# A transformer block on one core: the last products' snapshots and joins between the k tiles, and the gate g1 behind the output projection

## The chip, the core and the metric

The kernel runs on one core of a Trainium2 chip. A core has TensorE (PE in the rows) for matrix products, VectorE (DVE), ScalarE (ACT) and GpSimd (POOL) for the element work, and SyncE (SP), whose queue issues nearly all of the transfers between HBM and the on-chip memory SBUF here. Products collect in PSUM, in banks of 128 x 512 fp32. Each engine takes its instructions in a fixed order, and one that waits holds up all behind it on its engine. The metric is the time of one execution on the device, in microseconds.

## What is computed

A diffusion block on 1024 tokens of width 1024 in fp32. Cut to what matters here:

```python
mod = split(silu(c) @ w_ada + b_ada)            # sh1, sc1, g1, sh2, sc2, g2: one row of 1024 each
y   = sigmoid(ga) * (a_out @ w_branch_a) + sigmoid(gb) * (b_out @ w_branch_b)
x   = x + g1 * (y @ w_out)                      # output projection
h   = modulate(rmsnorm(x, norm2_g), sh2, sc2)
a, g = split(h @ w_ffn_in)                      # 1024 -> 2 x 2816
x   = x + g2 * ((silu(g) * a) @ w_ffn_out)      # 2816 -> 1024
return rmsnorm(x, final_norm_g)
```

Ahead of it stand the input projection, a gated linear attention (b_out) and a grouped MLP (a_out), which the change does not touch.

## The kernel before, in words

**High and low parts.** TensorE's fast fp32 form is coarser than fp32, so each operand X is split: `hi` is a rounded copy of X (a cast on ScalarE, L228 or L907) and `lo` is X - hi (a subtraction on VectorE, L229 or L908). A product is three matmuls, hi x hi, hi x lo and lo x hi (`PASS`). So each weight tile goes through a transfer (SyncE), a cast, a subtraction, and only then TensorE. `split_w` does that for weights, `parts_of` (L907, L908) for the tiles of the FFN.

**Who sets the order.** The program is written engine-free and a scheduler lays the instructions of each engine down in one fixed stream, roughly in the order in which the code emits them, as far as the buffers of the pools are free. Matmuls passed through `pe()` keep the program's order among themselves. So what is emitted early stands early in the queues of ScalarE, VectorE and SyncE, whether or not its inputs are there.

**Branch units and w_out.** For each of eight column blocks `fo`, a unit of 48 matmuls (L265) computes the gate, and another one a_out @ w_branch_a. At `fo` = 6 the row of g1 is spread over all partitions (`row_of`, L693 and L694), and `out_weights(0)` loads half of w_out in four tiles, multiplies each with that row (L837, two on GpSimd, two on VectorE) and splits them. The raw tiles come from the same small pool as the tiles of w_branch_a, so the load of the last unit waits until one of them is split. `project` then makes 24 matmuls per token tile and half (L880) and adds the result to x (L881). The second half is loaded by `out_weights(1)` in the same way. Behind each second half the token tile is normalised, and the transposed tiles feed the FFN.

**FFN in.** 22 blocks `fi` of 128 columns. A two-by-two block form with seven products stands for the eight, on sums of the weight's four quarters (S1 to S4, built in `weights_s`, L955 to L958) and of the activations. Behind each product stands element work that combines them (L987 to L1007); the results go to HBM (`actd`).

**FFN out.** Again seven products, P1, P7, P2, P6, P5, P4, P3 in this order, each over 11 k tiles (`quarter`, L1099 to L1101; P3 apart, L1166 to L1170). `prepared` loads a k tile's operands one ahead, combines them (L1074 to L1087) and splits them; a k tile is then 12 matmuls into four banks. All but P3 go k tile by k tile; P3 goes bank by bank, so its first bank wants all 11 tiles. Between the products stands the following, each piece for four token tiles:

- behind P1 and P7: a snapshot of the four banks by ScalarE (L1111, L1115)
- behind P2: `join`, that is multiply by the row of g2 and add to x (L1129, L1130)
- behind P6: add, subtract, multiply, add (L1138 to L1141)
- behind P5: add and `join` (L1158)
- behind P4: add, `join` and `finish`, the last normalisation (L1162, L1145 to L1154)
- behind each bank of P3: `join` and `finish`

In before all of it is emitted behind the product's last k tile and ahead of the next product's first. The row of g2 is made behind the loop over `fi`.

Of the kernel before, what the change touches and what calls it, by code (L numbers as in the profile page):

```python
# [1 line left out]

# [6 lines left out]
F32 = mybir.dt.float32  # L9
# [7 lines left out]
P = 128  # L17
T = 1024
TC = 256
D = 1024  # L20
# [12 lines left out]
def block_kernel(  # L33
# [796 lines left out]
    def out_weights(n):  # L830

        cols = slice(n * 512, (n + 1) * 512)
        parts = []
        for kp in range(KT // 2):
            raw = raw_w([P, 2, 512])
            nc.sync.dma_start(raw, w_out[kp * 256:(kp + 1) * 256, cols].rearrange("(k p) f -> p k f", p=P))
            (nc.vector if kp % 2 else nc.gpsimd).tensor_mul(raw, raw, g1r[:, cols].unsqueeze(1).to_broadcast([P, 2, 512]))  # L837
            parts.append(split_w(raw, [P, 2, 512], pool=True))
        return parts

# [29 lines left out]
    def project(n, tt, wo):  # L870
        cols = slice(n * 512, (n + 1) * 512)
        if n == 0:
            xt = slot([P, D])
            nc.sync.dma_start(xt, x[tt * P:(tt + 1) * P, :])
            x2.append(xt)
        xt = x2[tt]
        ps = bank()
        for k in range(KT):
            for i, (a, b) in enumerate(PASS):
                pe(nc.tensor.matmul(ps, yF.get(b, k, tt * P, P), wo[k // 2][a][:, k % 2, :], start=k == 0 and i == 0, stop=k == KT - 1 and i == 2))  # L880
        nc.vector.tensor_add(xt[:, cols], xt[:, cols], ps)  # L881
        if n == 1:
            xn = slot([P, D])
            rms_scaled(xt, xn)
            xns.append(xn)
            nc.sync.dma_start(x2d[tt], xt)
# [53 lines left out]
    def weights(fi, which=(0, 1)):  # L940
        got = []
        for i in which:
            w = raw_w([P, KT, P])
            nc.sync.dma_start(w, w_ffn_in[:, i * DFF + fi * P:i * DFF + (fi + 1) * P].rearrange("(k p) f -> p k f", p=P))
            got.append(w)
        return got

    def weights_a(va):
        hi, lo = split_w(va, [P, KT, P])
        return {"A11": (hi[:, 0:4, :], lo[:, 0:4, :]), "A12": (hi[:, 4:8, :], lo[:, 4:8, :])}  # L950
# [33 lines left out]
    def second(q):  # L984
        product(q["A"], q["ops"]["A12"], op_t["B21"], False)
# [43 lines left out]
    op_t["T1"] = moving(combined("tensor_sub", b12, b11, dve))  # L1029
    op_t["T4"] = moving(combined("tensor_sub", b21, t2, dve))  # L1030
    op_t["B22"] = moving(b22)
    for fi in range(NF):
        if fi < EARLY:
            if fi:
                weights_s(*weights(fi), quads[fi]["ops"], nc.vector)
            rest(quads[fi], fi)
        else:
            va, ga = weights(fi)
            q = {"ops": weights_a(va)}
            weights_s(va, ga, q["ops"], nc.gpsimd)  # L1040
            first(q)
            rest(q, fi, lambda: second(q))


    g2r = row_of(g2)
    sk = [slot([P, 2, 512]) for _ in range(KH // 2 + 1)]

    def act_q(k, t):
# [45 lines left out]
            t, now = operands(name, k + 1) if k + 1 < KH else None, t  # L1094
            yield parts_of(now)

    def quarter(name, banks, start):
        for k, o in enumerate(prepared(name)):
            for tt in range(4):  # L1099
                for i, (a, b) in enumerate(PASS):  # L1100
                    pe(nc.tensor.matmul(banks[tt], o[b][:, 0, tt * P:(tt + 1) * P], o[a][:, 1, :], start=start and k == 0 and i == 0, stop=k == KH - 1 and i == 2, skip_group_check=True))  # L1101

    def four():
        t = [slot([P, 2, 512]) for _ in range(2)]
        return [t[i // 2][:, i % 2, :] for i in range(4)]

    A, X = [gbank() for _ in range(4)], [bank() for _ in range(4)]
    quarter("P1", A, True)
    p1 = four()
    for tt in range(4):  # L1110
        nc.scalar.copy(p1[tt], A[tt])  # L1111
    quarter("P7", X, True)
    q7 = four()
    for tt in range(4):
        nc.scalar.copy(q7[tt], X[tt])  # L1115
    quarter("P2", A, False)
    fin = []
    fng, junkt = slot([P, D]), slot([P, 2, 512])
    junk = junkt[:, 0, :]
    nc.gpsimd.dma_start(fng, final_norm_g.partition_broadcast(P))  # L1120

    def residual(tt):
        xt = slot([P, D])
        nc.sync.dma_start(xt, x2d[tt])
        fin.append(xt)

    def join(xt, sl, src):
        t = tmp("gj")
        nc.vector.tensor_mul(t, src, g2r[:, sl])  # L1129
        nc.vector.tensor_add(xt[:, sl], xt[:, sl], t)  # L1130

    for tt in range(4):
        residual(tt)
        join(fin[tt], lh, A[tt])
    quarter("P6", X, False)
    u3 = four()
    for tt in range(4):
        nc.vector.tensor_add(u3[tt], X[tt], p1[tt])  # L1138
        nc.vector.tensor_sub(q7[tt], u3[tt], q7[tt])
        nc.vector.tensor_mul(q7[tt], q7[tt], g2r[:, rh])  # L1140
        nc.vector.tensor_add(fin[tt][:, rh], fin[tt][:, rh], q7[tt])  # L1141
    Y = [gbank() for _ in range(4)]
    quarter("P5", Y, True)

    def finish(tt):  # L1145
        xt = fin[tt]
# [6 lines left out]
            nc.vector.scalar_tensor_tensor(xt[:, sl], xt[:, sl], r[:, 0:1], fng[:, sl], op0=ALU.mult, op1=ALU.mult)  # L1153
            nc.sync.dma_start(out[tt * P:(tt + 1) * P, sl], xt[:, sl])  # L1154

    for tt in range(4):
        residual(4 + tt)
        nc.vector.tensor_add(u3[tt], Y[tt], u3[tt])  # L1158
        join(fin[4 + tt], rh, u3[tt])
    quarter("P4", X, False)  # L1160
    for tt in range(4):
        nc.vector.tensor_add(p1[tt], X[tt], p1[tt])  # L1162
        join(fin[4 + tt], lh, p1[tt])
        finish(4 + tt)

    o = list(prepared("P3"))  # L1166
    for tt in range(4):
        for k in range(KH):
            for i, (a, b) in enumerate(PASS):
# [35 lines left out]
```

## Time and profile before

| what | value |
|---|---|
| median of three runs | 1830.47 us (1828.61 to 1831.2) |
| the profiled execution | 1830.24 us |
| its span, first to last instruction | 1828.5 us |
| mean granted TensorE clock | 0.989 of full |
| w_branch_a's last unit ends, projection begins | 1058.59 us |
| FFN in ends, P1's first matmul | 1587.02 us |
| first matmul of P7, P2, P5, P3 | 1623.36, 1658.38, 1719.38, 1790.31 us |
| last matmul, end of span | 1820.41, 1828.5 us |

The profile is of one execution. Times are microseconds from the span's start. A timeline row gives a run of instructions of one form: its start, its length, the engine, the line, out <- in with partitions x elements, the count, and in brackets how long the engine had stood idle and what it waited for. Matmuls overlap, so the rate is read from the starts of rows and not from their lengths. The chain of waits is followed back from the last instruction: at each step the piece that released the next.

### The profile page before, as it was taken

The page shows a single profiled execution, that of the slowest core. Times are in us where ns is not written, and L with a number is a line of the kernel's source. Part 1 is how long each engine was busy: PE and PEld are TensorE (multiplying, and loading weights), DVE is VectorE, ACT ScalarE, POOL GpSimd, SP SyncE. Part 2 cuts the span into 40 slices and gives each one's busy share as a digit, 9 for nine tenths or more (in the row PEclk, how much of TensorE's full clock was granted, in tenths as well). Part 3 has the DMA queues.
Part 4 walks back from the last instruction along what each step waited for, and adds up shares of the span by engine and source line. Part 5 has one row for each costly group of instructions (what it writes and reads, how often), then busy time and mean ns, then how long its engine had stood idle before and what let it go on. Part 6 is the DMA issues. An engine that isn't in the chain of part 4 may idle for free.

```text
span 1828.5 us, 21986 instructions
## 1 busy us (share of the span) xinstructions
PE 1770.2 (97%) x8786; PEld 1478.2 (81%) x8786; DVE 982.2 (54%) x1386; ACT 600.4 (33%) x892; POOL 147.4 (8%) x145
## 2 busy tenths in 40 slices
PE   8899999999999999999999999989999999999898
PEld 3887888888887889988888788768888888777686
DVE  7687463553346525543322453885555455446786
ACT  6653342423211112132211222533333333345243
POOL 2220000000000000000000100011211211000001
PEclk9999999999999999999999999999999999999899
DMA  9501001011156448611111251242222222467382
GB/s 344 148 24 35 24 24 46 13 35 35 47 149 188 146 136 318 238 47 47 38 55 47 70 172 69 70 127 81 92 81 76 86 81 92 162 219 256 108 297 92
DMA packets 182870, 201.84 MB, mean 110 GB/s; under 512 B 8624, under 2 KB 132592, under 8 KB 182768
## 3 DMA queue, kind: packets, MB, share of 16 engines
q1 hardware_dynamic: 181952, 199.01, 33.6%
q0 software_dynamic: 720, 1.40, 0.3%
q8 instruction: 69, 1.13, 0.2%
q14 instruction: 33, 0.27, 0.0%
q10 hardware_dynamic: 96, 0.02, 0.0%
HBM read 168.94 MB, written 31.46 MB: 110 GB/s over the span
## 4 chain that ended last, share of the span: by engine, by line
PE 71%; DVE 4%; DMA 1%; issue 1%; ACT 1%; POOL 0%; DVEq 0%; POOLq 0%; ACTq 0%
PE m L265 28%; PE m L971 14%; PE g L971 6%; PE g L1101 5%; PE m L277 5%; PE m L1101 5%; PE m L880 5%; PE g L1170 2%; DVE s L908 1%; PE g L799 1%; DMA wr<-in_w_ffn_in_dram 1%; DVE s L916 0%; PE g L681 0%; DMA wr<-in_w_branch_a_dram 0%; DVE wlo L229 0%
## 5 line engine op out<-in xcount | busy, mean ns | idle before, releaser
L265 PE MATMUL m<-s,whi 128*128 128x512 f32 (+1 forms) x1856 | 571.5, 389 | 3.8 <-ACT whi L228 3.2
L265 PEld LDWEIGHTS m<-s,whi 128*128 128x128 f32 x1856 | 347.9, 189 | 75.3 <-ACT whi L228 4.1
L265 PE MATMUL m<-s,wlo 128*128 128x512 f32 (+1 forms) x928 | 360.1, 388 | 2.3 <-DVE wlo L229 2.3
L971 PE MATMUL m<-s,s 128*128 128x512 f32 x1320 | 309.5, 391 | 8.7 <-ACT q L991 3.8
L229 DVE TENSOR_TENSOR wlo<-wr,whi 128x1024 fp32r<-128x1024 f32 x106 | 129.7, 1225 | 344.7 <-ACT whi L228 311.8
L971 PEld LDWEIGHTS m<-s,s 128*128 128x128 f32 x1320 | 248.1, 189 | 64.1 <-ACT q L991 5.5
L228 ACT CAST whi<-wr 128x1024 fp32r<-128x1024 f32 x106 | 111.4, 1051 | 445.3 <-PE m L265 311.3
L277 PE MATMUL m<-whi,s 128*128 128x256 f32 x1152 | 218.1, 287 | 0.1
L265 PEld LDWEIGHTS m<-s,wlo 128*128 128x128 f32 x928 | 175.5, 189 | 37.6 <-DVE wlo L229 2.9
L277 PEld LDWEIGHTS m<-whi,s 128*128 128x128 f32 x1152 | 181.3, 192 | 4.5 <-issue 2.9
L277 PE MATMUL m<-wlo,s 128*128 128x256 f32 x576 | 164.4, 285 | 1.6 <-DVE wlo L229 1.6
L908 DVE TENSOR_TENSOR s<-wr,s 128x1024 fp32r<-128x1024 f32 x77 | 91.3, 1218 | 40.9 <-ACT s L907 40.4
L277 PEld LDWEIGHTS m<-wlo,s 128*128 128x128 f32 x576 | 110.2, 191 | 3.5 <-DVE wlo L229 2.0
L971 PE MATMUL g<-s,whi 128*128 128x512 f32 x352 | 108.4, 389 | 0.0
L907 ACT CAST s<-wr 128x1024 fp32r<-128x1024 f32 x77 | 78.3, 1050 | 60.5 <-DVE wr L1082 30.1
L1101 PE MATMUL g<-s,s 128*128 128x512 f32 x264 | 84.4, 402 | 11.3 <-DVE s L908 11.3
L908 DVE TENSOR_TENSOR s<-s,s 128x1024 fp32r<-128x1024 f32 x58 | 89.9, 1563 | 3.9 <-ACT s L907 3.9
L907 ACT CAST s<-s 128x1024 fp32r<-128x1024 f32 x58 | 60.4, 1053 | 89.0 <-DVE s L908 43.8
L880 PE MATMUL m<-s,s 128*128 128x512 f32 x384 | 87.5, 389 | 0.0
L1101 PE MATMUL m<-s,s 128*128 128x512 f32 x264 | 83.5, 398 | 0.7 <-DVE s L908 0.7
L880 PEld LDWEIGHTS m<-s,s 128*128 128x128 f32 x384 | 72.0, 188 | 14.9
L164 POOL TENSOR_TENSOR rstd<-rstd,nhalf 128x1 f32<-128x1 f32 (+2 forms) x43 | 27.8, 647 | 697.2 <-DVE rstd L163 697.1
(250 smaller groups left out, 2110.8 us busy)
## 6 DMA issues: line engine op xcount, KB each, us to landing
wr<-in_w_in_dram SPq DMA_DIRECT2D x68, 512.0 KB
wr<-in_w_ffn_in_dram SPq DMA_DIRECT2D x48, 512.0 KB
wr<-actd SPq DMA_DIRECT2D x77, 256.0 KB
wr<-in_w_ada_dram SPq DMA_DIRECT2D x32, 512.0 KB
s<-in_w_ffn_out_dram SPq DMA_DIRECT2D x22, 512.0 KB
wsT<-s SPq DMA_DIRECT2D x44, 256.0 KB
wr<-wsT SPq DMA_DIRECT2D x44, 256.0 KB
wr<-in_w_ffn_out_dram SPq DMA_DIRECT2D x33, 256.0 KB
```

Of the source, the lines that this page charges most:

```text
L164: nc.gpsimd.tensor_tensor(r[:, :n], r[:, :n], nhalf[:, :n], op=ALU.pow)
L228: nc.scalar.copy(hi, raw)
L229: lo_sub[0] = nc.vector.tensor_sub(lo, raw, f(hi)).ins
L265: nc.tensor.matmul(ps, ws[a][:, k, :], get(b, k, t0, n), start=k == 0 and i == 0, stop=k == nk - 1 and i == 2)
L277: nc.tensor.matmul(ps[:, j, :], get(b, 4 * kh + k, (2 * tp + j) * P, P), ws[a][:, k, :], start=kh == 0 and j == 0 and k == 0 and i == 0, s ...
L799: nc.tensor.matmul(pm[:, j, :], vg[g // 2][hf][:, j, (g % 2) * P:(g % 2) * P + P], wspT[:, g, :], start=j == 0, stop=True, skip_group_chec ...
L880: pe(nc.tensor.matmul(ps, yF.get(b, k, tt * P, P), wo[k // 2][a][:, k % 2, :], start=k == 0 and i == 0, stop=k == KT - 1 and i == 2))
L907: nc.scalar.copy(hi, raw)
L908: nc.vector.tensor_sub(lo, raw, f(hi))
L971: pe(nc.tensor.matmul(ps, wts[a][:, k, :], mov[k // 2][b][:, k % 2, :], start=start and k == 0 and i == 0, stop=k == 3 and i == 2, skip_gr ...
L1101: pe(nc.tensor.matmul(banks[tt], o[b][:, 0, tt * P:(tt + 1) * P], o[a][:, 1, :], start=start and k == 0 and i == 0, stop=k == KH - 1 and i ...
L1170: pe(nc.tensor.matmul(Y[tt], o[k][b][:, 0, tt * P:(tt + 1) * P], o[k][a][:, 1, :], start=False, stop=k == KH - 1 and i == 2, skip_group_ch ...
```

## The change

1. `out_weights` no longer multiplies the raw tiles of w_out by g1's row. `project` multiplies its result in PSUM by that row and then adds it: 16 operations of 128 x 512 on VectorE come in, four of 128 x 1024 on VectorE and four on GpSimd go.
2. `quarter` gets a list `side` of small pieces and emits `per` of them behind each k tile from the second on. The snapshot of P1 is emitted between the k tiles of P7, that of P7 between those of P2, the joins of P2 between those of P6, and so on. P3's tiles are all prepared ahead of its matmuls; the joins of P4 are emitted between them from the third tile on.
3. The row of g2 and the preparation of P1's first k tile are emitted behind `fi` = 20 and no longer behind the whole loop (`fi` = 21).

The line numbers move by one or two (L907 becomes L909, L908 L910, L955 L957, L971 L973) and in the last part by more: the matmuls of `quarter` are L1109, those of P3 L1196, `join` L1128 and L1129, the add behind P6 L1166, behind P4 L1182, `finish` L1135 to L1140.

```diff
@@ -834,7 +835,6 @@
         for kp in range(KT // 2):
             raw = raw_w([P, 2, 512])
             nc.sync.dma_start(raw, w_out[kp * 256:(kp + 1) * 256, cols].rearrange("(k p) f -> p k f", p=P))
-            (nc.vector if kp % 2 else nc.gpsimd).tensor_mul(raw, raw, g1r[:, cols].unsqueeze(1).to_broadcast([P, 2, 512]))
             parts.append(split_w(raw, [P, 2, 512], pool=True))
         return parts
@@ -878,7 +878,9 @@
         for k in range(KT):
             for i, (a, b) in enumerate(PASS):
                 pe(nc.tensor.matmul(ps, yF.get(b, k, tt * P, P), wo[k // 2][a][:, k % 2, :], start=k == 0 and i == 0, stop=k == KT - 1 and i == 2))
-        nc.vector.tensor_add(xt[:, cols], xt[:, cols], ps)
+        t = small.tile([P, 512], F32, tag="raw", name=nm("g1p"), bufs=4)
+        nc.vector.tensor_mul(t, ps, g1r[:, cols])
+        nc.vector.tensor_add(xt[:, cols], xt[:, cols], t)
         if n == 1:
             xn = slot([P, D])
             rms_scaled(xt, xn)
@@ -1029,20 +1031,7 @@
     op_t["T1"] = moving(combined("tensor_sub", b12, b11, dve))
     op_t["T4"] = moving(combined("tensor_sub", b21, t2, dve))
     op_t["B22"] = moving(b22)
-    for fi in range(NF):
-        if fi < EARLY:
-            if fi:
-                weights_s(*weights(fi), quads[fi]["ops"], nc.vector)
-            rest(quads[fi], fi)
-        else:
-            va, ga = weights(fi)
-            q = {"ops": weights_a(va)}
-            weights_s(va, ga, q["ops"], nc.gpsimd)
-            first(q)
-            rest(q, fi, lambda: second(q))
-    g2r = row_of(g2)
     sk = [slot([P, 2, 512]) for _ in range(KH // 2 + 1)]
     def act_q(k, t):
@@ -1094,53 +1083,50 @@
             t, now = operands(name, k + 1) if k + 1 < KH else None, t
             yield parts_of(now)
-    def quarter(name, banks, start):
-        for k, o in enumerate(prepared(name)):
+    gen, early = prepared("P1"), []
+    for fi in range(NF):
+        if fi < EARLY:
+            if fi:
+                weights_s(*weights(fi), quads[fi]["ops"], nc.vector)
+            rest(quads[fi], fi)
+        else:
+            va, ga = weights(fi)
+            q = {"ops": weights_a(va)}
+            weights_s(va, ga, q["ops"], nc.gpsimd)
+            first(q)
+            rest(q, fi, lambda: second(q))
+            if fi == NF - 2:
+                g2r = row_of(g2)
+                early = [next(gen)]
+    def quarter(gen, banks, start, side=(), per=2):
+        side = list(side)
+        for k, o in enumerate(gen):
             for tt in range(4):
                 for i, (a, b) in enumerate(PASS):
                     pe(nc.tensor.matmul(banks[tt], o[b][:, 0, tt * P:(tt + 1) * P], o[a][:, 1, :], start=start and k == 0 and i == 0, stop=k == KH - 1 and i == 2, skip_group_check=True))
+            if k >= 1:
+                for _ in range(per):
+                    if side:
+                        side.pop(0)()
+        for s in side:
+            s()
     def four():
         t = [slot([P, 2, 512]) for _ in range(2)]
         return [t[i // 2][:, i % 2, :] for i in range(4)]
-    A, X = [gbank() for _ in range(4)], [bank() for _ in range(4)]
-    quarter("P1", A, True)
-    p1 = four()
-    for tt in range(4):
-        nc.scalar.copy(p1[tt], A[tt])
-    quarter("P7", X, True)
-    q7 = four()
-    for tt in range(4):
-        nc.scalar.copy(q7[tt], X[tt])
-    quarter("P2", A, False)
-    fin = []
-    fng, junkt = slot([P, D]), slot([P, 2, 512])
-    junk = junkt[:, 0, :]
-    nc.gpsimd.dma_start(fng, final_norm_g.partition_broadcast(P))
     def residual(tt):
         xt = slot([P, D])
         nc.sync.dma_start(xt, x2d[tt])
-        fin.append(xt)
+        return xt
     def join(xt, sl, src):
         t = tmp("gj")
         nc.vector.tensor_mul(t, src, g2r[:, sl])
         nc.vector.tensor_add(xt[:, sl], xt[:, sl], t)
-    for tt in range(4):
-        residual(tt)
-        join(fin[tt], lh, A[tt])
-    quarter("P6", X, False)
-    u3 = four()
-    for tt in range(4):
-        nc.vector.tensor_add(u3[tt], X[tt], p1[tt])
-        nc.vector.tensor_sub(q7[tt], u3[tt], q7[tt])
-        nc.vector.tensor_mul(q7[tt], q7[tt], g2r[:, rh])
-        nc.vector.tensor_add(fin[tt][:, rh], fin[tt][:, rh], q7[tt])
-    Y = [gbank() for _ in range(4)]
-    quarter("P5", Y, True)
     def finish(tt):
         xt = fin[tt]
@@ -1153,17 +1139,57 @@
             nc.vector.scalar_tensor_tensor(xt[:, sl], xt[:, sl], r[:, 0:1], fng[:, sl], op0=ALU.mult, op1=ALU.mult)
             nc.sync.dma_start(out[tt * P:(tt + 1) * P, sl], xt[:, sl])
-    for tt in range(4):
-        residual(4 + tt)
+    fin, got = {}, {}
+    def later(fn, *tiles):
+        return [lambda tt=tt: fn(tt) for tt in range(4)]
+    A, X = [gbank() for _ in range(4)], [bank() for _ in range(4)]
+    quarter(itertools.chain(early, gen), A, True)
+    p1 = four()
+    quarter(prepared("P7"), X, True, later(lambda tt: nc.scalar.copy(p1[tt], A[tt])), 1)
+    q7 = four()
+    quarter(prepared("P2"), A, False, later(lambda tt: nc.scalar.copy(q7[tt], X[tt])), 1)
+    fng, junkt = slot([P, D]), slot([P, 2, 512])
+    junk = junkt[:, 0, :]
+    nc.gpsimd.dma_start(fng, final_norm_g.partition_broadcast(P))
+    def c11(tt):
+        fin[tt] = residual(tt)
+        join(fin[tt], lh, A[tt])
+    quarter(prepared("P6"), X, False, later(c11), 1)
+    u3 = four()
+    Y = [gbank() for _ in range(4)]
+    def u3_of(tt):
+        nc.vector.tensor_add(u3[tt], X[tt], p1[tt])
+    def u2_of(tt):
+        nc.vector.tensor_sub(q7[tt], u3[tt], q7[tt])
+        join(fin[tt], rh, q7[tt])
+    quarter(prepared("P5"), Y, True, later(u3_of) + later(u2_of), 1)
+    def c22(tt):
+        fin[4 + tt] = residual(4 + tt)
         nc.vector.tensor_add(u3[tt], Y[tt], u3[tt])
         join(fin[4 + tt], rh, u3[tt])
-    quarter("P4", X, False)
-    for tt in range(4):
+    quarter(prepared("P4"), X, False, later(c22), 1)
+    def c21(tt):
         nc.vector.tensor_add(p1[tt], X[tt], p1[tt])
         join(fin[4 + tt], lh, p1[tt])
         finish(4 + tt)
-    o = list(prepared("P3"))
+    side = later(c21)
+    o = []
+    for k, parts in enumerate(prepared("P3")):
+        o.append(parts)
+        if k >= 2 and side:
+            side.pop(0)()
     for tt in range(4):
         for k in range(KH):
             for i, (a, b) in enumerate(PASS):
```

What this does to the queues is shown at three places. The rows are a queue's instructions in order: line, operation, out <- in, size; `s` are tiles of SBUF, `wr` raw operands, `g` and `m` PSUM banks, `u`, `p`, `q` the combined products of a block `fi`.

VectorE around `fi` = 20, before. L955 and L956 are sums for the last block (`fi` = 21), L1006 and L1007 end block 18, L908 on `s` are the low parts of such sums:

```order
L955 TENSOR_TENSOR s_11640<-wr_11632,wr_11634 128x512
L1006 TENSOR_TENSOR q_1663_11290<-m_11289,q_1663_11290 128x512
L965 TENSOR_TENSOR s_11526<-wr_11506,s_11526 128x512
L1007 TENSOR_TENSOR q_1663_11290<-q_1663_11290,u_1664_11291 128x512
L956 TENSOR_TENSOR s_11640<-wr_11634,s_11640 128x512
L229 TENSOR_TENSOR wlo_11637<-wr_11632,whi_11636 128x1024
L995 TENSOR_TENSOR u_1681_11419<-m_11416,p_1677_11414 128x512
L908 TENSOR_TENSOR s_11647<-s_11640,s_11646 128x1024
L998 TENSOR_TENSOR u_1681_11419<-m_11417,u_1681_11419 128x512
```

The same place after; L1008 and L1009 end block 20, L695 are the two row copies of g2, L910 on `wr` is P1's first tile, and L957, L958 and L910 on `s` are for block 21:

```order
L997 TENSOR_TENSOR u_1720_11577<-m_11574,p_1716_11572 128x512
L1000 TENSOR_TENSOR u_1720_11577<-m_11575,u_1720_11577 128x512
L1003 TENSOR_TENSOR p_1716_11572<-m_11574,p_1716_11572 128x512
L1005 TENSOR_TENSOR p_1716_11572<-p_1716_11572,g_11559 128x512
L1008 TENSOR_TENSOR q_1719_11576<-m_11575,q_1719_11576 128x512
L1009 TENSOR_TENSOR q_1719_11576<-q_1719_11576,u_1720_11577 128x512
L695 COPY s_11662<-g_11663 128x512
L695 COPY s_11662<-g_11669 128x512
L910 TENSOR_TENSOR s_11682<-wr_11675,s_11681 128x1024
L957 TENSOR_TENSOR s_11693<-wr_11685,wr_11687 128x512
L958 TENSOR_TENSOR s_11693<-wr_11687,s_11693 128x512
L910 TENSOR_TENSOR s_11700<-s_11693,s_11699 128x1024
```

The sums of block 21 stood while block 18 ended, and now stand behind the end of block 20, the row copies and P1's tile.

VectorE from P6 to P5, before. L1082 combines P5's operands, L1138 to L1141 are the joins of P6; P5's first low part follows the last of these:

```order
L1082 TENSOR_TENSOR wr_12770<-wr_12770,s_11774 128x512
L1082 TENSOR_TENSOR wr_1903_12790<-wr_1903_12790,s_11774 128x512
L1082 TENSOR_TENSOR wr_12810<-wr_12810,s_11775 128x512
L1082 TENSOR_TENSOR wr_1909_12830<-wr_1909_12830,s_11775 128x512
L1082 TENSOR_TENSOR wr_1915_12870<-wr_1915_12870,s_11776 128x512
L1138 TENSOR_TENSOR s_12724<-m_11783,s_11996 128x512
L1138 TENSOR_TENSOR s_12724<-m_11784,s_11996 128x512
L1139 TENSOR_TENSOR s_12255<-s_12724,s_12255 128x512 x2
L1140 TENSOR_TENSOR s_12255<-s_12255,s_11760 128x512 x2
L1141 TENSOR_TENSOR s_12473<-s_12473,s_12255 128x512
L1141 TENSOR_TENSOR s_12478<-s_12478,s_12255 128x512
```

The same place after; L1071 combines P5's operands, L910 are P5's low parts, L1166 is the first add of P6's joins:

```order
L910 TENSOR_TENSOR s_12763<-wr_12754,s_12762 128x1024
L1071 TENSOR_TENSOR wr_12778<-wr_12778,s_9114 128x512
L910 TENSOR_TENSOR s_12783<-wr_1913_12758,s_12782 128x1024
L1071 TENSOR_TENSOR wr_1919_12799<-wr_1919_12799,s_9114 128x512
L1071 TENSOR_TENSOR wr_12820<-wr_12820,s_9115 128x512
L1071 TENSOR_TENSOR wr_1925_12841<-wr_1925_12841,s_9115 128x512
L1071 TENSOR_TENSOR wr_12862<-wr_12862,s_9116 128x512
L1071 TENSOR_TENSOR wr_1932_12886<-wr_1932_12886,s_9116 128x512
L1071 TENSOR_TENSOR wr_1940_12934<-wr_1940_12934,s_9117 128x512
L1166 TENSOR_TENSOR s_12748<-m_11817,s_12020 128x512
L1166 TENSOR_TENSOR s_12748<-m_11818,s_12020 128x512
L910 TENSOR_TENSOR s_12804<-wr_12778,s_12803 128x1024
```

Two of P5's low parts stand ahead of the joins now, and the third behind two of them.

VectorE from P4 to P3, before. L1087 and L908 alternate over P3's 11 tiles, L1162 is the first of P4's joins:

```order
L908 TENSOR_TENSOR s_13324<-wr_2001_13311,s_13323 128x1024
L1087 TENSOR_TENSOR wr_2007_13327<-wr_2007_13327,s_11777 128x512
L908 TENSOR_TENSOR s_13332<-wr_13319,s_13331 128x1024
L1087 TENSOR_TENSOR wr_13335<-wr_13335,s_11778 128x512
L908 TENSOR_TENSOR s_13340<-wr_2007_13327,s_13339 128x1024
L908 TENSOR_TENSOR s_13344<-wr_13335,s_13343 128x1024
L1162 TENSOR_TENSOR s_11996<-m_11783,s_11996 128x512
L1162 TENSOR_TENSOR s_11996<-m_11784,s_11996 128x512
L1129 TENSOR_TENSOR gj_13200<-s_11996,s_11760 128x512
L1129 TENSOR_TENSOR gj_13215<-s_11996,s_11760 128x512
```

The same place after; L1076 combines P3's operands, L1182, L1128, L1129 and L1139 belong to P4's joins and `finish`, the two last L910 are tiles 9 and 10 of P3:

```order
L1076 TENSOR_TENSOR wr_2027_13355<-wr_2027_13355,s_9117 128x512
L910 TENSOR_TENSOR s_13360<-wr_13347,s_13359 128x1024
L1182 TENSOR_TENSOR s_12020<-m_11817,s_12020 128x512
L1182 TENSOR_TENSOR s_12020<-m_11818,s_12020 128x512
L1128 TENSOR_TENSOR gj_13256<-s_12020,s_11662 128x512
L1128 TENSOR_TENSOR gj_13279<-s_12020,s_11662 128x512
...
L1076 TENSOR_TENSOR wr_13363<-wr_13363,s_9118 128x512
L1139 SCALAR_TENSOR_TENSOR s_13085<-s_13085,rstd_13309,s_12494 128x512 x2
L1136 TENSOR_TENSOR ss_13328<-ss_13328 128x1
L910 TENSOR_TENSOR s_13368<-wr_2027_13355,s_13367 128x1024
L164 TENSOR_SCALAR rstd_13332<-ss_13328 128x1
L910 TENSOR_TENSOR s_13372<-wr_13363,s_13371 128x1024
```

The other nine of P3's low parts stand ahead of P4's joins, and the last two behind nearly all of them.

## Rows read from the trace of the kernel before

**Rows 1.** The page's busy time of each engine: us, share of the span, instructions.
```profile
PE 1770.2 (97%) x8786; PEld 1478.2 (81%) x8786; DVE 982.2 (54%) x1386; ACT 600.4 (33%) x892; POOL 147.4 (8%) x145
```

**Rows 2.** TensorE's waits: engine, line, releaser; us in total, times, longest.
```profile
PE g L1101 <- DVE s L908: 11.3, 3, 8.7
...
PE m L265 <- ACT whi L228: 3.2, 1, 3.2
```

**Rows 3.** TensorE's timeline, start of P1: start, us, line, operation [idle before <- releaser].
```profile
1585.32 1.95 PE L693 MATMUL g<-ident,mod 128*128 128x128 f32 x16
...
1587.02 0.47 PE L1101 MATMUL g<-s 128*128 128x512 f32 x1
...
1593.07 0.63 PE L1101 MATMUL g<-s,s 128*128 128x512 f32 x2
```

**Rows 4.** TensorE's timeline, from P1 to P7.
```profile
1620.28 0.61 PE L1101 MATMUL g<-s,s 128*128 128x512 f32 x2
...
1630.66 0.40 PE L1101 MATMUL m<-s 128*128 128x512 f32 x1
```

**Rows 5.** TensorE's timeline, last branch unit and first projection matmul.
```profile
1041.61 0.39 PE L265 MATMUL m<-s,wlo 128*128 128x512 f32 x1
...
1058.59 1.75 PE L880 MATMUL m<-s,s 128*128 128x512 f32 x7
```

**Rows 6.** The chain of waits, 1028 to 1060 us: start, us, what.
```profile
1031.09 3.37 POOL wr L837
...
1035.56 3.48 DVE s L229 x2
...
1039.06 4.94 DMA wr<-in_w_branch_a_dram
...
1044.07 1.05 ACT whi L228
```

**Rows 7.** The chain of waits, 1583 to 1600 us.
```profile
1585.52 0.70 DVE q L1006
...
1588.05 1.22 DVE s L908
```

**Rows 8.** One window: busy us by engine, then TensorE's granted clock, DMA share, GB/s.
```profile
1625.00:1630.00 5.00, 5.00 (x13) 3.84 (x13) 3.53 (x4) 5.00 (x8) 0.00 (x0) 0.50 0.78 245
```

**Rows 9.** TensorE's timeline, from P7 to P2.
```profile
1656.77 0.61 PE L1101 MATMUL m<-s,s 128*128 128x512 f32 x2
...
1660.21 0.39 PE L1101 MATMUL g<-s 128*128 128x512 f32 x1
```

**Rows 10.** TensorE's timeline, from P6 to P5.
```profile
1719.38 0.39 PE L1101 MATMUL g<-s 128*128 128x512 f32 x1
...
1728.52 1.22 PE L1101 MATMUL g<-s,s 128*128 128x512 f32 x2 [8.75 <-DVE s L908]
...
1733.18 0.40 PE L1101 MATMUL g<-s 128*128 128x512 f32 x1
```

**Rows 11.** The chain of waits, 1712 to 1740 us, one of eight such pairs.
```profile
1718.92 1.20 DVE s L1139 x2
```

**Rows 12.** The chain of waits, 1148 to 1158 us.
```profile
1150.05 5.45 PE g L971 x24
```

**Rows 13.** VectorE's timeline, behind the last projection matmul.
```profile
1152.87 0.75 DVE L173 TENSOR_SCALAR s<-s,rstd 128x1024 f32<-128x1024 f32 x1 [0.73 <-POOL rstd L164]
```

**Rows 14.** VectorE's timeline, a low part beside GpSimd in the FFN-in loop.
```profile
1540.14 2.33 DVE L908 TENSOR_TENSOR s<-s,s 128x1024 fp32r<-128x1024 f32 x1 [0.17 <-ACT s L907]
```

**Rows 15.** GpSimd's timeline, same place.
```profile
1540.10 1.28 POOL L996 TENSOR_TENSOR q<-u,q 128x512 f32<-128x512 f32 x1 [6.07 <-ACT s L907]
```

**Rows 16.** VectorE's timeline, joins of P4: first and last of the run.
```profile
1788.47 1.37 DVE L1162 TENSOR_TENSOR s<-m,s 128x512 f32<-128x512 f32 x2
...
1800.64 1.42 DVE L1153 SCALAR_TENSOR_TENSOR s<-s,rstd,s 128x512 f32<-128x512 f32 x2
```

**Rows 17.** TensorE's timeline, first matmul of P3.
```profile
1790.31 0.39 PE L1170 MATMUL g<-s 128*128 128x512 f32 x1
```

More of the change, by code (lines that the diff above doesn't have):

```diff
@@ L1 @@
+import itertools
 from contextlib import ExitStack
```

## Prediction

> **What bounds the kernel now.** I read the page's busy times first [rows 1]: TensorE is busy 97% of the span, every other engine far less. So the reader should ask only where TensorE stands still or runs below its full clock. The list of TensorE's waits answers that: its largest entry is the FFN-out loop's matmuls (L1101) waiting for VectorE's low part (L908), 11.3 us in 3 waits, one of them 8.7 us, and the branch units wait once 3.2 us for a cast [rows 2]. TensorE's own timeline then gives, place by place, what such a wait costs together with the lower clock behind it. The measure is the steady rate: from 1593.07 to 1620.28 [rows 3, 4] 120 matmuls take 27.21 us, 0.2268 us each, so a k tile of 12 takes 2.72 and a product of 132 takes 29.9.
>
> **What the change removes.** I count the matmuls between two rows and subtract their time at that rate.
> - Front (w_out times g1): 49 matmuls from 1041.61 to 1058.59 [rows 5] take 16.98 us instead of 11.11: 5.9 lost. The chain shows why [rows 6]: the GpSimd multiply of L837 (3.37), a cast, two low parts of L229 (3.48 together), and only then is the load of the last w_branch_a block issued, at 1039.06; it takes 4.94, its cast 1.05. Without L837 the same cast starts when g1's row would have been ready, 3.37 earlier, and the low parts no longer run beside a GpSimd multiply (3.48 for two becomes 2 x 1.22 by [rows 7]), another 1.0. The load is issued near 1034.7, cast and low part end near 1042.0, and TensorE needs them at 1041.84 and 0.23 later. The whole 5.9 goes.
> - Start of P1: 10 matmuls from 1587.02 to 1593.07 [rows 3] take 6.05 instead of 2.27: 3.8. They wait for the first low part, which stands behind the last block's two operations (L1006, L1007) and the two row copies of g2 [rows 7]; of the 3.8, 2.07 are idle (1587.25 to 1589.32) and 1.7 are clock. After the change that tile is prepared one block earlier, and several more stand ahead of the last block's operations. All 3.8 goes.
> - P1 to P7: 17 matmuls from 1620.28 to 1630.66 [rows 4] take 10.38 instead of 3.86: 6.5. Some of it is clock: from 1625 to 1630 TensorE was granted half speed, 1.2 GHz of 2.4, after standing still [rows 8]. The four snapshots of P1 stand on ScalarE ahead of P7's first casts; now two of P7's k tiles are cast ahead of them.
> - P7 to P2: 5 matmuls from 1656.77 to 1660.21 [rows 9] take 3.44 instead of 1.13: 2.3, from the same cause.
> - P6 to P5: 12 matmuls from 1719.38 to 1733.18 [rows 10] take 13.80 instead of 2.72: 11.1, of it 8.9 idle and 2.2 clock. In between VectorE does eight pairs of joins at 1.20 us a pair [rows 11] and only then the second half of P5's first tile. By the new order the first two tiles' low parts are issued ahead of the joins and two more after the first pair; two tiles are 5.44 us of matmuls, the pair ahead 1.2. All 11.1 goes.
> The other boundaries of before (P2 to P6, P5 to P4, P4 to P3) show no gap. Sum of the gains: 5.9 + 3.8 + 6.5 + 2.3 + 11.1 = 29.6.
>
> **What it adds.** Sixteen multiplies of a PSUM result by g1, one 128x512 VectorE operation each (0.70 by a like one [rows 7]), 11.2 us of VectorE in the projection. They lengthen only the path from the last projection matmul to the transposes, by 0.7: there TensorE has 5.45 us of block products (from 1150.05), while the normalised tile is scaled at 1152.87 in 0.75 us; it has then 1.9 us to spare [rows 12, 13]. At nothing; 0.7 to 1.4 if that cover is gone. The four multiplies of the raw weights that go from VectorE pay back some of it.
>
> **What it moves: two new waits.** Both come from code that is emitted earlier than what the next TensorE work needs, so that it stands in front of it in VectorE's queue.
> (a) Block fi=20 to 21. In before the sums for fi=21 (L955, L956) stand more than two blocks ahead. Now they stand behind the two operations of block 20, the two row copies and P1's first low part. That is the very sequence the chain shows at 1585.52 to 1589.27 [rows 7], 3.78 after the end of the products. Call the end of block 20's products Z: sums end Z+5.1 (0.70 + 0.60), their cast Z+6.2 (1.05 by [rows 6]), the low part Z+7.5 (1.22). TensorE has in the meantime g2's row (1.70 from 1585.32 to 1587.02 [rows 3]) and product A11 of 12 matmuls (2.72), to Z+4.4, plus two matmuls on the high part (0.45): idle 2.6. The low part here runs beside two GpSimd sums, though, and such a one took 2.33 [rows 14] next to a GpSimd operation of 1.28 [rows 15]: then idle 3.7. Clock: nothing, or 1.7 as at P1's start, or up to 2.9. The bounds are 2.6 and 6.6; I take 3.7 + 1.7 = 5.4, since the P1 start is the nearest row in sequence and in size.
> The Trainium skill (SBUF — State Buffer, Who interferes with whom) says that a VectorE instruction with two SBUF inputs contends with a GpSimd instruction that reads SBUF, and that whoever issues first holds the port for the whole instruction; rows 14 and 15 agree, 2.33 for what takes 1.22 alone. By that rule the low part would start only after both GpSimd sums, and the sum below would be longer by some 0.4; without it shorter by 1.1.
> (b) P4 to P3. P3 runs bank by bank, so its first bank wants all 11 tiles within 33 matmuls, 7.5 us. In before all eleven low parts stand ahead of the joins of P4. Now the last two (k=9 and 10) stand behind all of them: four L1182, four multiplies, four adds and six of the scalings in finish. In before this run takes VectorE from 1788.47 to 1802.06 [rows 16], with P3's first matmul at 1790.31 [rows 17], T. So k=9 has its low part at 1802.06 + 1.22, T+13.0, and k=10 at T+14.1. TensorE does 28 matmuls to T+6.35, idles 6.6, does three more and idles another 0.5: 7.1. Clock behind it: 2.2 as at P6 to P5, the nearest in length of idling [rows 10]. I take 9.3. Low end 6.4 (the first join cannot start before its bank is done, 2.0 before T, and no clock lost); high end 10.5 (VectorE still 0.5 behind on tile 8, clock 2.9).
>
> **The sum.** The profiled execution took 1830.24 us (span 1828.5 and 1.74 around it), 0.2 under the median of 1830.47. 1830.24 - 29.6 + 5.4 + 9.3 = 1815.3.
>
> **Rivals.**
> 1. The new waits are small: VectorE gets through joins faster than in before, or the clock holds. With 2.6 and 6.4 the time is 1830.2 - 29.6 + 9.0 = 1809.6. For it: most of what I charge as clock is read from other places. Against it: the order of the queue is fixed and the join run's length is a row.
> 2. Neither wait shows: 1800.6. It would need idle VectorE time that rows 16 does not show.
> 3. The front does not do what it says: the load of w_branch_a comes no earlier in time to help, because something else on SyncE's queue or its buffer holds it. Then 5.9 stay: 1821.2. Against it: in the chain the load follows the L229 that frees its buffer within 0.02 us.
> 4. P6 to P5 stays blocked, since tile 3 onwards waits behind the joins: 11.1 stay, 1826.4, hardly to be told from no change (a measurement of this kernel tells 0.2% or 3.7 us).
> 5. Slower: the joins block every boundary as I expect at P3. The place is the head of VectorE's and ScalarE's queues at P1-P7, P7-P2, P2-P6, P6-P5 and P5-P4; the price is P3's 9.3 each, 46.5 in place of the 19.9 that these boundaries cost before: 1830.2 - 9.7 - 19.9 + 46.5 + 14.7 = 1861.8. It decides where the tiles prepared ahead times 2.72 fall short of the joins ahead. By the order two or more tiles stand ahead everywhere, 5.44 against 1.2 to 2.4 of joins before the next low part, so it is unlikely.
>
> **How the numbers follow.** Forecast 58% (its own range 1811 to 1819: the bounds of (a) and (b) and the small terms), rival 1 15%, rival 2 5%, rival 3 10%, rival 4 6%, rival 5 6%. The range 1807 to 1823 takes in the forecast and rivals 1 and 3, 83%. Faster by over 0.2%: 58 + 15 + 5 + 10 = 88%; within 0.2%: 6%; slower: 6%.
>
> **What would show it.** Right: in the list of TensorE's waits the 8.7 us wait of the FFN-out loop is gone, and two new ones stand there, S3 of fi=21 (product L973 on the sums' cast and low part, 3 to 4 us) and P3's first bank (L1196 on L910, some 7 us in its first 14 us). The gaps at 1042, 1587, 1621, 1657 and 1719 are closed. Wrong: a wait of more than a microsecond at P7, P2, P6, P5 or P4's start; P3's first bank without a gap; or the cast of the last w_branch_a block still over a microsecond late.

## The result, and the profile after

The changed kernel takes 1818.49 us (median of four runs, 1817.76 to 1818.85) against 1830.84 for the kernel before in the same comparison: ratio 0.9934, 95% interval [0.9917, 0.9951]. It is faster, by some 12.3 us or 0.7%; forecast were 1815.3 us, a gain of 14.9 by its sum (15.2 under the median of before that it had). The profiled execution took 1818.25 us, its span 1816.5.

I cut both traces at the same TensorE instructions. Each number is the difference of two row starts (the first counts from the span's start, the last to its end):

| stretch | before | after | gain | forecast |
|---|---|---|---|---|
| start to g1's row | 1029.14 | 1030.17 | -1.0 | 0 |
| g1's row to first projection matmul | 29.45 | 23.58 | 5.9 | 5.9 |
| projection, to the first FFN-in product behind it | 91.30 | 92.11 | -0.8 | 0 |
| FFN in, to P1 | 437.13 | 442.97 | -5.8 | -5.4 |
| P1 to P3's first matmul | 203.29 | 180.48 | 22.8 | 23.7 |
| P3 to the end | 38.19 | 47.19 | -9.0 | -9.3 |
| span | 1828.5 | 1816.5 | 12.0 | 14.9 |

The first line is chance: in the ten profiles of this case it lies between 1028.93 and 1030.56, and the code up to there is the same.

The page's busy times after, for [rows 1]: TensorE has 7.1 us less with the same number of matmuls, and the mean granted clock rose from 0.989 to 0.994, so fewer of them ran at the lower clock; GpSimd has lost its four multiplies.

```profile
PE 1763.1 (97%) x8786; PEld 1472.8 (81%) x8786; DVE 982.9 (54%) x1398; ACT 599.3 (33%) x892; POOL 137.5 (8%) x141
```

The last branch unit runs through; TensorE after, for [rows 5]:

```profile
1053.52 0.39 PE L266 MATMUL m<-s,wlo 128*128 128x512 f32 x1
1053.75 2.43 PE L880 MATMUL m<-s,s 128*128 128x512 f32 x10
```

The load of the last w_branch_a block is issued 4.97 us behind g1's row (1030.17), where [rows 6] have it 9.92 behind (1039.06 from 1029.14). SyncE's timeline, after:

```profile
1035.14 0.37 SPq L254 DMA_DIRECT2D wr<-in_w_branch_a_dram  x1
```

TensorE's waits after (engine, line, releaser; us in total, times, longest), those that answer to [rows 2] and those that are new:

```profile
PE g L1196 <- DVE s L910: 7.3, 1, 7.3
...
PE m L973 <- DVE u L997: 2.3, 1, 2.3
...
PE m L973 <- ACT s L909: 1.7, 1, 1.7
...
PE g L1109 <- DVE p L1005: 0.7, 1, 0.7
...
PE g L899 <- ACT s L904: 0.6, 1, 0.6
...
PE g L899 <- DVE s L902: 0.5, 1, 0.5
```

The 11.3 us of the FFN-out loop and the 3.2 of the branch unit are gone. The first entry is the prediction's (b), P3's first bank. The third is the first half of (a), at block 21. The others I had not priced: L997, L1005, and two waits at the first transposes (L899).

The three boundaries that had a gap (P1 to P7, P7 to P2, P6 to P5) closed completely. P7 follows P1 at the steady rate (0.45 us for the two matmuls ahead of its first), where [rows 4] show 10.38 us for 17; P5 follows P6 alike, where [rows 10] show 8.75 of waiting. TensorE's timeline after, at P7's and at P5's first matmul:

```profile
1619.26 0.61 PE L1109 MATMUL g<-s,s 128*128 128x512 f32 x2
1619.71 0.39 PE L1109 MATMUL m<-s 128*128 128x512 f32 x1
```

```profile
1709.02 0.61 PE L1109 MATMUL m<-s,s 128*128 128x512 f32 x2
1709.47 0.39 PE L1109 MATMUL g<-s 128*128 128x512 f32 x1
```

From P7 to P3 five products take 29.92 us each.

At P3 the forecast wait is there: 7.35 us where 7.1 was forecast. TensorE, then VectorE at the same place, both after:

```profile
1769.31 0.39 PE L1196 MATMUL g<-s 128*128 128x512 f32 x1
...
1775.43 0.39 PE L1196 MATMUL g<-s 128*128 128x512 f32 x1
1783.17 1.22 PE L1196 MATMUL g<-s,s 128*128 128x512 f32 x2 [7.35 <-DVE s L910]
```

```profile
1768.04 1.28 DVE L1182 TENSOR_TENSOR s<-m,s 128x512 f32<-128x512 f32 x2
...
1781.90 1.22 DVE L910 TENSOR_TENSOR s<-wr,s 128x1024 fp32r<-128x1024 f32 x1
```

The joins begin 1.3 us ahead of P3's first matmul (T = 1769.31), tile 9's low part ends at T+13.8 where I had T+13.0. The idling also cost clock, which is why the stretch lost 9.0: counted at the steady rate, 7.5 of standing still and 1.5 of clock. One window each, after: TensorE's granted clock is the first number behind the five engines; half is 1.2 GHz of 2.4.

```profile
1565.00:1570.00 5.00, 2.52 (x11) 1.46 (x10) 3.62 (x4) 1.56 (x2) 2.58 (x2) 1.00 0.31 109
...
1780.00:1785.00 5.00, 1.83 (x4) 1.41 (x5) 4.12 (x8) 1.86 (x5) 1.92 (x2) 0.50 0.34 129
```

The first window is block 21: there TensorE stood 1.71 us and 0.78 us and kept its full clock. I had charged 1.7 for it. TensorE after, block 21 to P1:

```profile
1561.91 1.95 PE L694 MATMUL g<-ident,mod 128*128 128x128 f32 x16
1563.61 0.71 PE L973 MATMUL g<-s,whi 128*128 128x512 f32 x2
...
1568.32 0.73 PE L973 MATMUL m<-s,s 128*128 128x512 f32 x2 [1.71 <-ACT s L909]
1569.83 2.56 PE L973 MATMUL m<-s,s 128*128 128x512 f32 x10 [0.78 <-DVE s L910]
1572.22 0.61 PE L973 MATMUL g<-s,whi 128*128 128x512 f32 x2
...
1582.95 6.04 PE L973 MATMUL m<-s,s 128*128 128x512 f32 x24 [2.27 <-DVE u L997]
...
1588.83 0.39 PE L1109 MATMUL g<-s 128*128 128x512 f32 x1
...
1591.69 0.50 PE L1109 MATMUL g<-s 128*128 128x512 f32 x1 [0.66 <-DVE p L1005]
```

From the row of g2 (1561.91, 1.70 long) to P1, 84 matmuls at 0.2268 would take 19.05; 26.92 - 1.70 - 19.05 = 6.2 are lost. Up to the product behind S3 (1572.22) it is 3.2, and 3.0 come at the second wait, on L997, with another 1.0 inside P1 (30.88 for 29.92). VectorE, then ScalarE, both after, say what L997 waits behind:

```profile
1581.07 1.23 DVE L910 TENSOR_TENSOR s<-wr,s 128x1024 fp32r<-128x1024 f32 x1 [2.67 <-ACT s L909]
1582.21 0.68 DVE L997 TENSOR_TENSOR u<-m,p 128x512 f32<-128x512 f32 x1
```

```profile
1579.99 3.92 ACT L909 CAST s<-wr 128x1024 fp32r<-128x1024 f32 x4 [3.19 <-DMA wr<-in_w_ffn_out_dram]
```

L997 joins block 21's own product. Ahead of it in the queue stands the low part of one of P1's tiles, whose load and cast had not come. It is the same fault as (a) and (b), at a third place.

### The profile page after: what moved, and what is told of

Read it like the earlier page. It is cut to its first block, busy times and chain, and to the rows that moved or that the text cites. A ratio compares the mean times of both kernels' runs of the same rounds, so it can differ in the third digit from the quotient of the medians.

```text
span 1816.5 us, 22024 instructions
## 1 busy us (share of the span) xinstructions
PE 1763.1 (97%) x8786; PEld 1472.8 (81%) x8786; DVE 982.9 (54%) x1398; ACT 599.3 (33%) x892; POOL 137.5 (8%) x141
## 5 line engine op out<-in xcount | busy, mean ns | idle before, releaser
L973 PE MATMUL m<-s,s 128*128 128x512 f32 x1320 | 309.5, 391 | 14.2 <-DVE s L910 4.0
L973 PEld LDWEIGHTS m<-s,s 128*128 128x128 f32 x1320 | 246.5, 188 | 71.4 <-ACT q L993 5.8
L973 PE MATMUL g<-s,whi 128*128 128x512 f32 x352 | 108.5, 390 | 0.0
L910 DVE TENSOR_TENSOR s<-wr,s 128x1024 fp32r<-128x1024 f32 x77 | 91.1, 1218 | 28.9 <-ACT s L909 28.8
L909 ACT CAST s<-wr 128x1024 fp32r<-128x1024 f32 x77 | 78.6, 1054 | 51.3 <-DVE wr L1071 19.0
L910 DVE TENSOR_TENSOR s<-s,s 128x1024 fp32r<-128x1024 f32 x58 | 89.1, 1548 | 6.8 <-ACT s L909 6.8
L909 ACT CAST s<-s 128x1024 fp32r<-128x1024 f32 x58 | 60.5, 1053 | 88.2 <-DVE s L910 41.0
L880 PEld LDWEIGHTS m<-s,s 128*128 128x128 f32 x384 | 72.0, 188 | 14.9
L1109 PE MATMUL g<-s,s 128*128 128x512 f32 x264 | 81.2, 389 | 0.0
L1109 PE MATMUL m<-s,s 128*128 128x512 f32 x264 | 81.2, 389 | 0.0
```

The lines of the kernel that those rows point to most:

```text
L909: nc.scalar.copy(hi, raw)
L910: nc.vector.tensor_sub(lo, raw, f(hi))
L973: pe(nc.tensor.matmul(ps, wts[a][:, k, :], mov[k // 2][b][:, k % 2, :], start=start and k == 0 and i == 0, stop=k == 3 and i == 2, skip_gr ...
```

## The experiments

The medians of these runs stand beside those of the kernel before in the same job: 1830.67 us for the first four, 1831.18 for the last four. The changed kernel was measured in another job, beside 1830.84; where a run is compared with it, the ratios to before would move the difference by up to 0.4 us.

**The g1 edit alone**, on the kernel before:

```diff
-            (nc.vector if kp % 2 else nc.gpsimd).tensor_mul(raw, raw, g1r[:, cols].unsqueeze(1).to_broadcast([P, 2, 512]))
...
-        nc.vector.tensor_add(xt[:, cols], xt[:, cols], ps)
+        t = small.tile([P, 512], F32, tag="raw", name=nm("g1p"), bufs=4)
+        nc.vector.tensor_mul(t, ps, g1r[:, cols])
+        nc.vector.tensor_add(xt[:, cols], xt[:, cols], t)
```

> The kernel before with the g1 edit alone (multiply behind the projection, not on the weights). My theory: the branch units lose their 5.9 us gap, the 16 multiplies cost 0.8 us where the projection's first eight transposes wait for PSUM banks that VectorE now frees later. Time: 5.1 us under before, 0.28%. TensorE's waits for the last w_branch_a cast (3.2) and low part (1.8) are gone, the two L899 waits (0.5 and 0.6) stand in their place. Rival (the multiplies are free and the 0.8 of the changed kernel came from something else): 5.9 us under before, no new wait at the transposes.

Measured: 1824.97 us, ratio 0.9966 [0.9954, 0.9979], 5.7 under before. The time lies between my 5.1 and the rival's 5.9 and does not decide; the trace does. The projection takes 92.11 us as in the changed kernel (before 91.30), and the first transposes wait as there; TensorE's timeline:

```profile
1132.11 0.66 PE L898 MATMUL g<-ident,s 128*128 128x128 f32 x4 [0.49 <-DVE s L901]
1133.37 1.53 PE L898 MATMUL g<-ident,s 128*128 128x128 f32 x12 [0.60 <-ACT s L903]
```

So the 0.8 belongs to the multiplies: the addition of a projection tile now ends 0.7 us later, and behind it stand VectorE's evacuations of the transposes' banks, and ScalarE's behind the norm that needs the sum. The branch unit's two waits are gone, 3.17 on the cast and 0.53 on the low part; the 1.8 that the expectation gives for the low part is another wait, at 59.7 us, and stays.

**Only the snapshots and joins between the k tiles**: the changed kernel with the diff above turned round, and the one of the run without the early part, below.

> The changed kernel without the g1 edit and without the early start of P1 (both as before): only the snapshots and joins between the k tiles. My theory: 6.5 + 2.3 + 11.1 = 19.9 us gained at P7, P2 and P5, 9.0 lost at P3: 10.9 us under before, 0.60%. TensorE keeps the waits of the branch unit (3.2) and P1's start (1.8), shows none at P7, P2, P6, P5, P4, and one of 7.3 at P3. Rival (part of the gain hangs on P1's early start, which shifts the k tiles ahead of the joins): a wait at P7 stays, gain under 8 us.

Measured: 1820.54 us, 0.9939 [0.9925, 0.9952], 10.1 under before. All stretches from P7 to P3 are 29.92, and the list of waits holds the branch unit's 3.2, P1's 1.8 and 7.4 at P3. The part needs neither of the other two, against the rival. P3 to the end takes 47.62, so the loss there is 9.4 in this execution.

**P3's tiles ahead of P4's joins**, the rest as changed:

```diff
-    side = later(c21)
-    o = []
-    for k, parts in enumerate(prepared("P3")):
-        o.append(parts)
-        if k >= 2 and side:
-            side.pop(0)()
+    o = list(prepared("P3"))
+    for s in later(c21):
+        s()
```

> The changed kernel, but P3's 11 tiles are emitted ahead of P4's joins, as in before. My theory (only the order in VectorE's queue makes the wait): P3 runs without a gap, 9.0 us under the changed kernel, near 1809.4. Rival (VectorE is full by then, the wait moves): the tiles are on time but the joins end later, the last bank's normalisation or P3's own first bank waits, gain 0 to 4 us.

Measured: 1809.59 us, 0.9885 [0.9871, 0.9899], 8.9 under the changed kernel. No L1193 (P3) entry is left among TensorE's waits, and P3 to the end takes 38.13, as before (38.19). VectorE's timeline:

```profile
1769.61 1.22 DVE L910 TENSOR_TENSOR s<-wr,s 128x1024 fp32r<-128x1024 f32 x1
1770.74 0.68 DVE L1182 TENSOR_TENSOR s<-m,s 128x512 f32<-128x512 f32 x1
1771.34 1.22 DVE L910 TENSOR_TENSOR s<-wr,s 128x1024 fp32r<-128x1024 f32 x1
```

Tile 10 is ready at 1772.56, 2.3 us behind P3's first matmul (1770.27) and 4.5 ahead of its own turn (30 matmuls, 6.8 us). VectorE was not full: the joins, now later, hold up nothing. The wait was the order alone.

**Without the early part**: `row_of(g2)` and P1's first tile behind the loop.

```diff
             rest(q, fi, lambda: second(q))
-            if fi == NF - 2:
-                g2r = row_of(g2)
-                early = [next(gen)]
+    g2r = row_of(g2)
```

> The changed kernel with the row of g2 and P1's first tile behind the whole loop, as in before. My theory (the early part pays less than it costs): the waits of block 21 go, 3.4 at its first sum product, 2.8 at the join L997 and 1.1 at P1's second bank group, and P1's start has its 3.8 back: 3.5 us under the changed kernel, near 1815. Rival (the blocked L997 comes from late loads of P1's tiles, whatever the order): the wait shows again inside P1, time within 1 us of the changed kernel or over it.

Measured: 1814.81 us, 0.9911 [0.9898, 0.9925], 3.7 under the changed kernel. TensorE's L973 no longer waits for L997 or L909, and P1's start waits 1.83 again:

```profile
1583.61 0.47 PE L1108 MATMUL g<-s 128*128 128x512 f32 x1
1585.92 0.50 PE L1108 MATMUL g<-s,s 128*128 128x512 f32 x1 [1.83 <-DVE s L910]
```

P1 takes 32.15, 2.2 too long, which is that wait and no other, against the rival; in the run with the joins alone, with the same wait, it took 33.75, 3.8 too long, as in before [rows 3]. The same 2 us of idling cost 1.6 us of clock in one execution and nothing in another.

From FFN in to P7 the two traces with the g1 edit and the early part behind the loop (this run and the both-repairs run below) need 470.8 and 469.1 us; three with it ahead of block 21 (changed, P3's tiles first, P5's joins first) 473.9, 476.0 and 475.3. Within each group the traces differ by the clock in a stretch that no edit touches. Between 1185 and 1210 us the granted clock fell below full in six of the ten profiled executions: in this run, P3's tiles first and P5's joins first, but not in the changed kernel nor in both repairs. One window of this run, then of both repairs:

```profile
1185.00:1190.00 5.00, 3.63 (x9) 2.94 (x10) 4.40 (x7) 2.27 (x3) 0.00 (x0) 0.66 0.00 0
```

```profile
1185.00:1190.00 5.00, 3.46 (x15) 2.55 (x14) 4.93 (x7) 1.78 (x3) 0.00 (x0) 1.00 0.00 0
```

Like with like, the third part of the change costs 4.8 us more than it saves (473.9 and 469.1), or 4.5 to 5.2 (476.0 and 475.3, 470.8), and 3.7 by the times. The joins alone, without the g1 edit, need 473.3; that execution had the deepest such fall and the 1.6 of clock at P1.

**P6's joins ahead of P5's tiles**, one boundary undone:

```diff
-    quarter(prepared("P5"), Y, True, later(u3_of) + later(u2_of), 1)
+    for tt in range(4):
+        u3_of(tt)
+        u2_of(tt)
+    quarter(prepared("P5"), Y, True)
```

> The changed kernel, but the joins of P6 are emitted in one piece ahead of P5's first tile, as in before. My theory (P6 to P5 alone is worth 11.1: 8.9 of idle TensorE behind sixteen joins and 2.2 of lower clock): 11.1 us over the changed kernel, near 1829.5, with a wait of 8.7 at P5's start. Rival (with the rest changed, P5's tiles are prepared far enough ahead anyway): no such wait, within 2 us of the changed kernel.

Measured: 1821.13 us, 0.9941 [0.9924, 0.9957]: only 2.6 over the changed kernel. My number was wrong, and the trace tells why. P5's wait is back in full, and P5 takes 40.64 instead of 29.92, 10.7 more. TensorE, then VectorE at P3, in this kernel:

```profile
1719.12 1.22 PE L1109 MATMUL g<-s,s 128*128 128x512 f32 x2 [8.75 <-DVE s L910]
```

```profile
1776.74 2.47 DVE L910 TENSOR_TENSOR s<-wr,s 128x1024 fp32r<-128x1024 f32 x2
1779.13 1.28 DVE L1185 TENSOR_TENSOR s<-m,s 128x512 f32<-128x512 f32 x2
```

P3's last two low parts stand ahead of P4's joins here, although the code of that place was not touched: P3 to the end takes 38.26, 8.9 less. The edit at P5 shifted where the scheduler lays the joins down one product and a half later. 10.7 - 8.9 = 1.8; the spans differ by 2.3, the rest being 1.5 more in FFN in, where the clock fell near 1195, and 1.0 less of chance at the start. The expectation had held the other places fixed.

**The early part inside the last block**, behind its sums and its first product and ahead of the other six:

```diff
+            if fi == NF - 1:
+                g2r = row_of(g2)
+                early = [next(gen)]
             rest(q, fi, lambda: second(q))
-            if fi == NF - 2:
-                g2r = row_of(g2)
-                early = [next(gen)]
```

> The changed kernel, with the row of g2 and P1's first tile emitted inside the last block, behind its weights' sums, and not ahead of them. My theory: the sums keep their place two blocks ahead, so the 3.4 us at block 21's first sum product go; P1's tiles 1 to 5 still stand ahead of block 21's join L997, so its wait of 2.3 to 2.6 stays: near 1815. Rival (the L997 wait is a consequence of the late sums, not of P1's tiles): it goes too, near 1811.

Measured: 1814.83 us, 0.9906 [0.9891, 0.9920]. The number is the expected one, the way there not. The L909 wait of block 21 is gone; so is the one on L997, and a smaller one on the next join, L1000, stands in its place, behind another of P1's tiles:

```profile
1582.76 3.01 PE L973 MATMUL m<-s,s 128*128 128x512 f32 x12 [0.94 <-DVE u L1000]
```

Neither theory had that. FFN in to P7 takes 470.2, with the fall of the clock near 1185, against 470.8 for no early part with the same fall. That is 0.6, which the times (1814.83 and 1814.81) do not tell.

**Both repairs**, the diffs of P3's tiles first and of no early part together:

> Both repairs that the runs point to: P3's tiles ahead of P4's joins, and the row of g2 and P1's first tile behind the loop. My theory (the two waits are independent): 9.0 + 3.5 under the changed kernel, near 1806, and no wait in the FFN-out loop over 2 us; P1's start keeps its 1.8. Rival (the two overlap, VectorE is full): near 1809.

Measured: 1804.01 us, 0.9849 [0.9834, 0.9864], 14.5 under the changed kernel's median, where 12.5 was expected. The wait at P3 and those of block 21 are gone together: the two repairs add up, against the rival. The stretches give 9.0 at P3 and 4.8 from FFN in to P7, neither with a fall of the clock near 1185. The rest is not explained; runs of one kernel lie up to 5 us apart (P3's tiles first, 1807.82 to 1812.78).

**P3's tiles first, and the early part inside the last block**, the two diffs together:

> P3's tiles ahead of P4's joins, and the early part inside the last block behind its sums. My theory: the first run of this group without the 9.0 at P3, so near 1806, level with the version that has no early part: what it saves at P1's start (2.1 idle, with clock up to 3.8) it pays at L997 (2.3 to 2.6). Rival (the L997 wait goes with the sums in place): near 1802.5, 3.5 under that version.

Measured: 1803.65 us, 0.9847 [0.9832, 0.9861]: the same as the run above within the measurement, as expected; but the way is not the expected one, since the wait on L997 is gone and 0.95 on L1000 stands. FFN in to P7 takes 468.5, 0.6 less than in the run above, as in the pair before. These two are the fastest versions, 1.5% under the kernel before. The last 0.8 at the transposes and 1.8 at P1's start (or 0.9 at L1000) I did not try to remove.

## Why the prediction was right, and where a size was off

- **What bounds it.** Right: every microsecond won or lost is TensorE standing still, or below its clock behind it, in front of a queue of VectorE or ScalarE.
- **Front.** Right, 5.9 of 5.9, and the branch unit needs no part of the rest (g1 alone). The load came 4.95 us earlier behind g1's row, for the 4.4 (3.37 + 1.0) of the prediction.
- **The multiplies "at nothing".** Wrong in size, 0 for 0.8. I had looked for cover at the transposes behind the last projection tile, where it holds: TensorE goes from the block products into them without a wait, with g1 alone as before. The place was one group of token tiles earlier, at the first 32 transposes, which need banks that VectorE and ScalarE clear behind the additions. I had named a bound of 0.7 to 1.4 for lost cover, and it covers the 0.8, at another place.
- **The boundaries and P1's start.** Right in mechanism. P1 to P3's start gained 22.8 of 23.7; the missing 0.9 is the wait on L1005 that P1's own tiles cause.
- **(a) Block 20 to 21.** The wait was there, nearer the size without GpSimd than the one with it: counted as the prediction counts, TensorE stands still 3.05 us, to 1569.83, where 2.6 and 3.7 were forecast (the profile gives 1.71 and 0.78 as idle). The terms of the forecast add up to Z+7.35 and not 7.5, but its 3.78 is 3.95 when counted from the start of g2's row (1585.32), so the 2.6 stands. I had taken 3.7 and 1.7 of clock, 5.4; it cost 3.2. No clock fell, and the low part did not wait for both GpSimd sums: it took 1.47, for 1.22 alone, and the second GpSimd sum beside it 2.28, where the first had taken 1.27:

```profile
1567.42 1.27 POOL L959 TENSOR_TENSOR s<-s,wr 128x512 f32<-128x512 f32 x1 [11.30 <-DVE s L958]
1568.64 2.28 POOL L960 TENSOR_TENSOR s<-wr,s 128x512 f32<-128x512 f32 x1
```

The Trainium skill (SBUF — State Buffer, Who interferes with whom) says that a VectorE instruction with two SBUF inputs contends with a GpSimd instruction that reads SBUF, that this is an exclusive lock, and that issue order decides who blocks. The rows agree within 0.2 us, with the parts exchanged: the low part, started at 1568.30 while the first sum still ran (to 1568.69), came ahead of the second, which was the one that lost 1.0. I had applied the rule as if both sums came first.

- **The step that failed** is the list of what the early part moves. I counted the sums of block 21 (a) and stopped there; the same edit also put P1's tiles ahead of block 21's joins, where they wait for loads. The prediction even says of those tiles that "several more stand ahead of the last block's operations", and counts that only as a gain for P1. That is 3.0 at L997 and 1.0 at L1005. With 0.8 at the transposes and 1.0 of chance at the start that makes 5.8 lost; 2.2 by which (a) was priced too high, 0.3 of (b) and 0.4 spread over the rest come back. The difference is the 2.9 between 14.9 and 12.0. That the stretch from FFN in to P1 lost 5.8 for a forecast of 5.4 is luck: 2.2 too much at (a) covers most of the 3.0 that was not on the list.
- **(b) P4 to P3.** Right, 9.0 of 9.3, and the repair gives it back (8.9). The parts are off both ways, 7.5 of standing still for 7.1 and 1.5 of clock for 2.2. In the three other profiled executions with this wait the stretch takes 47.62, 47.94 and 48.06, so 9.4 to 9.9 is lost. What the prediction did not see is that it hangs on more than the code at that place: undoing P6 to P5 removed it too.
- **Rivals.** 2 to 5 did not come. Rival 1 is half true: (a) was nearly as small as it said (3.2 for 2.6), (b) was not (9.0 for 6.4).

What stays open: why the scheduler lays P4's joins differently once P6's are in one piece. That it does is in the rows; its reason was not looked into.

## What to carry to other kernels

Work that is emitted between the steps of the next stage hides only as long as it stands behind what that stage needs first; a piece whose input comes late, put ahead of it in an engine's queue, stops everything behind it. So after such an edit go through the whole queue, not only the place edited, and ask of each moved piece what waits for a load or for another engine and who stands behind. And test one part at a time by the stretches of the trace, not by the total: here the total of one undone part (2.6) hid a loss of 10.7 and a gain of 8.9.

## What was not expected of the hardware

The same idling did not always cost clock. 2 us at P1's start cost 1.6 in two profiled executions (before, the joins alone) and nothing in three others (g1 alone, no early part, both repairs). The two that paid are those without the g1 edit; with one profile of each kernel, no run shows whether that is more than chance. In a stretch that no edit touches, TensorE stands 1.8, 0.2, 0.6, 1.5 and 2.5 to 2.7 us between 1173 and 1198 in all ten, and between 1185 and 1210 the clock fell in six and held in four. The 2.3 us at L997 left it full in the changed kernel; 2.6 us there in P3's tiles first were followed by 0.66 of full from 1585 to 1590. 2.5 us in two pieces at block 21 cost nothing, while 7.35 us at P3 brought the window from 1780 to 1785 to half the clock. An estimate for a wait of 2 us should therefore hold both.
